# Per-head sums and spreads in 32-wide strips of TensorE, in a RWKV-7 mixer

## The chip, the cores and the metric

The kernel runs on one core of a Trainium2 chip, in one launch. The metric is the device time in microseconds (us). Each run gives one time; a profiled execution gives the rows that are quoted here. The engines are TensorE (PE; its weight loads are PEld), VectorE (DVE), ScalarE (ACT), GpSimd (POOL) and SyncE (SP), which issues the loads. Each works through its own queue in order, and waits for others by semaphores.

## The reference

One decoder layer over 256 tokens of width 2048: a mixer (pooling heads beside RWKV-7 heads), an MLP of width 8192, a gated embedding and a last norm. What the change touches are two places in the RWKV-7 half, which has 16 heads of 64 channels:

```python
kk = hs(k * k_k)                                  # (B, T, H, 64)
kk = kk / jnp.maximum(jnp.linalg.norm(kk, axis=-1, keepdims=True), 1e-12)
...
y = wkv7_scan(r_h, hs(decay), k_h, v_h, -kk, kk * a_h)
...                                               # group norm of y
y = y + jnp.sum(r_h * k_h * r_k, axis=-1, keepdims=True) * v_h
```

Both are a sum over the 64 channels of a head, for each token, and a spread of a number per head and token back over those channels: the inverse norm of kk, and the bonus that multiplies v.

## The kernel before

Activations of the mixer lie with channels on the 128 partitions and the 256 tokens along the free axis, as tiles of four 128-channel blocks: `[128, 4, 256]`, two heads in each block. The 16 heads are done in two groups of eight (`gi` 0 and 1), so a group is one such tile.

Products of the big weights are made of fp32r matmuls: ScalarE makes a rounded high part `wh` of the weights (L163), VectorE the rest `wl` (L164), and three matmuls per tile add high and low parts. An fp32 matmul, which the mixer's small work uses, stands in the profile as two passes, each with its own weight load.

TensorE's order is the order in which the code is written. Generators of the big products (`zk`, `zr`, `zv`, the pool's `zp`, and part of the output product, `o0a` and on) stand in a queue, and `fill(us)` takes steps from its head until about so many microseconds of matmuls are written; a step of `zk`, `zr` or `zv` is put at 0.36, one of `zp` at 0.68. So each `fill` is cover for what the small work waits for. The other engines' order is made by a scheduler, which goes by priorities (`tc.high_priority`) and its own estimates of time. `inverse` (a triangular inverse on VectorE, 31 steps on `X` and `tmp` and then four transposes, L661 and L665) is written beside the products.

The banks of PSUM for the small work come from a ring of four (`rw_bank`); the next user of a bank waits for its last reader.

The norms, in `rwkv_k`: ScalarE squares (L512, tile `tF`), TensorE sums a head's channels with the squares as the weights and two columns of ones, `jhead` (L524, tile `kkn`), so that tokens come out on the partitions: 128 x 16 numbers. VectorE and ScalarE make the inverse root `rn` (L527 to L529), TensorE transposes it (L533, `rnT`), it is split in high and low parts (`rnp`), and TensorE spreads it with `hsel` (L543, L544, tile `rnb`); VectorE multiplies (L548). The split parts borrow the place of `k2` (tag `tE`), so `k2` is made after them.

The bonus, in `rwkv_values`: v is transposed and centred (L699, `vt`; copies to `UV` at L701), then `block_sum` sums and spreads in one, by a 128 x 128 block of ones `jsum` (L463, `bsum`), and VectorE multiplies by v (L706).

The calls stand in this order: `rwkv_k(0)`, `rwkv_r(0)`, `rwkv_scores(0)`, inverse of group 0 beside, `rwkv_lora(1)`, `rwkv_k(1)`, `rwkv_r(1)`, the rest of the inverse, `rwkv_values(0)`, `fill(7.0)`, `rwkv_scores(1)`, and later `rwkv_merge(1)`, `rwkv_values(1)`, `rwkv_core(1)`.

Of the kernel before, what the change touches and what calls it, by code (L numbers as in the profile page):

```python
# [9 lines left out]
F32 = mybir.dt.float32  # L10
F32R = mybir.dt.float32r
AF = mybir.ActivationFunctionType
ALU = mybir.AluOpType
# [3 lines left out]
T = 256  # L17
# [23 lines left out]
def trunk(  # L41
# [19 lines left out]
    nc = tc.nc  # L61
# [7 lines left out]
    mc = rctx.enter_context(tc.tile_pool(name="mc", bufs=1))  # L69
# [4 lines left out]
    def rw_bank(name):  # L74
        return psr.tile([128, 512], F32, tag="rw", name=name)
# [5 lines left out]
    def col(name, j):  # L81
        o = PARAM_COLS[name] + j
        return par_sb[:, o : o + 1]
# [12 lines left out]
    jsum = mc.tile([128, 128], F32, name="jsum")  # L96
# [4 lines left out]
    nc.gpsimd.tensor_copy(jsum, cmask)  # L101
    cen = mc.tile([128, 128], F32, name="cen")
    nc.vector.scalar_tensor_tensor(cen, jsum, -1.0 / 64.0, ident, op0=ALU.mult, op1=ALU.add)
    jhead = mc.tile([128, 2], F32, name="jhead")
    nc.gpsimd.tensor_copy(jhead, cmask[:, ::64])
# [61 lines left out]
    def split_sb(h_ap, l_ap, src_ap):  # L167
        nc.scalar.activation(h_ap, src_ap, AF.Copy)
        nc.vector.tensor_tensor(l_ap, src_ap, h_ap.bitcast(F32), op=ALU.subtract)
# [67 lines left out]
    def advance():  # L237
        try:
            us = next(queue[0])
            pace(us)  # L240
            return us
        except StopIteration:
            queue.pop(0)
            return 0.0

    def fill(us):

        while us > 0 and queue:
            us -= advance()
# [47 lines left out]
    hsel_f = rp.tile([8, 512], F32, tag="BKt", name="hsel_f")  # L297
    nc.gpsimd.memset(hsel_f, 1.0)
    nc.gpsimd.affine_select(hsel_f, hsel_f, [[1, 512]], ALU.is_ge, 0.0, base=0, channel_multiplier=-64)
    nc.gpsimd.affine_select(hsel_f, hsel_f, [[-1, 512]], ALU.is_ge, 0.0, base=63, channel_multiplier=64)  # L300
    hsel = mc.tile([8, 512], F32R, name="hsel")
    nc.gpsimd.tensor_copy(hsel, hsel_f)

    def flat(t_):
        return t_.rearrange("p a t -> p (a t)")
# [148 lines left out]
    def pair_tile(tag, name, **kw):  # L454
        t_ = rp.tile([128, 2, 512], F32R, tag=tag, name=name, **kw)
        return t_[:, 0, :], t_[:, 1, :]

    def block_sum(src, name, consume):

        s = flat(src)  # L460
        for hf in range(2):
            b = rw_bank("bsum")
            nc.tensor.matmul(b, jsum, s[:, hf * 512 : (hf + 1) * 512], start=True, stop=True)  # L463
# [43 lines left out]
    def rwkv_k(gi, st, zk):  # L507
        P, EI, aa = st["P"], st["EI"], st["aa"]
        sq, kkn, k2 = e4("tF"), e4("tB"), e4("tE")
        with tc.high_priority(30000):  # L510
            for p in range(4):
                nc.scalar.activation(sq[:, p, :], zk[:, p, :], AF.Square, scale=col("k_k", 4 * gi + p))  # L512
        nc.scalar.activation(warm, sq[:, 3, 0:1], AF.Sqrt)

        fill(5.4)
        nb = rw_bank("kkn")
        for hf in range(2):
            h = flat(sq)[:, hf * 512 : (hf + 1) * 512]
            for j in range(2):
                for tt in range(2):  # L520
                    o = tt * 8 + (2 * hf + j) * 2
                    ts_ = slice(j * T + tt * 128, j * T + (tt + 1) * 128)
                    first = hf == 0 and j == 0 and tt == 0
                    nc.tensor.matmul(nb[:, o : o + 2], h[:, ts_], jhead, start=first, stop=True, skip_group_check=True)  # L524
        rn = rp.tile([128, 16], F32, tag="rn", name=f"rn{gi}")
        with tc.high_priority(30000):
            nc.vector.tensor_scalar_max(rn, nb[:, 0:16], 1e-24)  # L527
# [4 lines left out]
        for tt in range(2):  # L532
            nc.tensor.transpose(nb[0:8, tt * 128 : (tt + 1) * 128], rn[:, tt * 8 : tt * 8 + 8], ident)  # L533
        rnh, rnl = (t_[0:8, 0:T] for t_ in pair_tile("tE", f"rnp{gi}"))
        with tc.high_priority(30000):
            split_sb(rnh, rnl, nb[0:8, 0:T])
        fill(1.8)
        for half in range(2):
            b = rw_bank("rnb")
            for j in range(2):  # L540
                p = half * 2 + j
                o = b[:, j * T : (j + 1) * T]
                nc.tensor.matmul(o, hsel[:, p * 128 : (p + 1) * 128], rnh, start=j == 0, stop=False, skip_group_check=True)  # L543
                nc.tensor.matmul(o, hsel[:, p * 128 : (p + 1) * 128], rnl, start=False, stop=True, skip_group_check=True)  # L544
            for j in range(2):
                p = half * 2 + j
                with tc.high_priority(30000):
                    nc.vector.scalar_tensor_tensor(  # L548
                        kkn[:, p, :], zk[:, p, :], col("k_k", 4 * gi + p), b[:, j * T : (j + 1) * T], op0=ALU.mult, op1=ALU.mult
                )  # L550
# [140 lines left out]

    def rwkv_values(gi, st, zv):

        uvs = [rp.tile([128, 2, 8, 64], F32, tag=f"q{i}", name=f"UV{gi}_{i}") for i in range(2)]
        UV = [uvs[c // 2][:, c % 2] for c in range(4)]
        for tt in range(2):
            b = rw_bank("vt")
            for p in range(4):
                nc.tensor.matmul(b[:, p * 128 : (p + 1) * 128], zv[:, p, tt * 128 : (tt + 1) * 128], cen, start=True, stop=True)  # L699
            for i in range(2):  # L700
                nc.scalar.activation(flat3(UV[2 * tt + i])[64:128], b[i * 64 : (i + 1) * 64, :], AF.Copy)  # L701
        bon = st["rk"]
        bf, vf = flat(bon), flat(zv)
        block_sum(
            st["rk"], f"rk{gi}",
            lambda hf, b: nc.vector.tensor_tensor(  # L706
                bf[:, hf * 512 : (hf + 1) * 512], b, vf[:, hf * 512 : (hf + 1) * 512], op=ALU.mult
            ),
        )
        st["UV"] = UV  # L710

    def rwkv_core(gi, st):
# [88 lines left out]
    def flat3(t_):  # L801
        return t_.rearrange("s h i -> s (h i)")
# [588 lines left out]
```

## Time and profile before

| | us |
|---|---|
| median of 3 runs | 1205.14 (1204.48 to 1205.86) |
| profiled execution | 1204.86 |
| its span, first to last instruction | 1203.1 |
| TensorE busy | 1183.2 |
| VectorE busy | 872.9 |
| ScalarE busy | 674.7 |
| GpSimd busy | 15.5 |

The times of the profile count from the start of the span. A row of the order in time has start, duration, engine, line, operation, tiles (written from read), shapes and how many it merges; in square brackets stands how long the engine was idle before it and what ended that. Matmuls are pipelined: what one costs is the distance to the start of the next, not its duration. The mixer lies between 25 and 340 us, the first group's norms near 60, the second group's near 141 to 151, the values of the groups at 164 and 269.

### The profile page before, as it was taken

How to read it: one execution, taken by the hardware profiler on the slowest of the kernel's cores; microseconds unless marked ns; L12 is line 12 of the kernel's file. 1: busy time of each engine (PE TensorE's matmuls, PEld its weight loads, DVE VectorE, ACT ScalarE, POOL GpSimd, SP SyncE). 2: the span in 40 equal slices, each digit the busy share in tenths (PEclk: the TensorE clock that was granted, in tenths of full speed). 3: DMA queues.
4: the chain of work that ended last, by engine and by line, in shares of the span. 5: the costliest groups of instructions: out<-in, count | busy, mean ns of one | idle time of the engine just before them, and what ended most of it. 6: DMA issues, size and time to landing. Idle time of an engine off the chain costs nothing.

```text
span 1203.1 us, 18401 instructions
## 1 busy us (share of the span) xinstructions
PE 1183.2 (98%) x7070; PEld 1015.0 (84%) x7070; DVE 872.9 (73%) x1186; ACT 674.7 (56%) x1203; POOL 15.5 (1%) x65
## 2 busy tenths in 40 slices
PE   7999999999999999999999999999999999999997
PEld 5999988987888888888888888888888887887886
DVE  6887987964566666666878887666667788788753
ACT  5957556565545545555545554555555555468743
POOL 3100000000000000000000000000000000000000
PEclk9999999999999999999999999999999999999999
DMA  7363543354365565565656666665565666666841
GB/s 275 124 195 113 175 141 107 107 187 142 120 211 175 175 192 184 185 191 180 192 200 205 206 194 217 185 191 181 187 192 168 194 205 204 229 203 200 271 139 70
DMA packets 60616, 216.88 MB, mean 180 GB/s; under 512 B 6768, under 2 KB 7536, under 8 KB 60144
## 3 DMA queue, kind: packets, MB, share of 16 engines
q1 hardware_dynamic: 60240, 215.20, 55.5%
q8 instruction: 55, 0.90, 0.3%
q10 hardware_dynamic: 288, 0.51, 0.1%
q14 instruction: 33, 0.27, 0.1%
HBM read 213.59 MB, written 2.10 MB: 179 GB/s over the span
## 4 chain that ended last, share of the span: by engine, by line
PE 89%; DVE 6%; DMA 2%; ACT 2%; issue 1%; ACTq 0%; DVEq 0%
PE u_w L1016 20%; PE d_p L1085 15%; PE u_w L1020 10%; PE d_w L1085 4%; PE d_d L1085 4%; DMA raw_d<-in_w_ffn_down_dram 2%; PE gt_b L187 2%; PE gt_b L186 2%; PE gt_b L185 2%; PE wag_b L346 1%; PE zp_b L185 1%; PE zv_b L176 1%; PE zp_b L187 1%; PE zp_b L186 1%; PE o_b L186 1%; PE o_b L185 1%
## 5 line engine op out<-in xcount | busy, mean ns | idle before, releaser
L1016 PE MATMUL u_w<-h,wh_u 128*128 128x512 f32 x1024 | 362.1, 399 | 0.0
L1020 PE MATMUL u_w<-h,wl_u 128*128 128x256 f32 x1024 | 287.7, 281 | 0.0
L164 DVE TENSOR_TENSOR wl_u<-raw_u,wh_u 128x1024 fp32r<-128x1024 f32 x128 | 156.7, 1224 | 122.2 <-ACT wh_u L163 122.2
L163 ACT ACTIVATE wh_u<-raw_u 128x512 fp32r<-128x512 f32 x256 | 147.6, 624 | 173.4 <-issue 137.0
L1016 PEld LDWEIGHTS u_w<-h,wh_u 128*128 128x128 f32 x1024 | 192.4, 188 | 47.9
L1020 PEld LDWEIGHTS u_w<-h,wl_u 128*128 128x128 f32 x1024 | 193.4, 189 | 0.0
L1085 PE MATMUL d_p<-wh_d,yd 128*128 128x512 f32 x480 | 154.5, 389 | 0.8 <-ACT wh_d L163 0.8
L163 ACT ACTIVATE wh_d<-raw_d 128x512 fp32r<-128x512 f32 x160 | 89.1, 620 | 36.8 <-issue 18.5
L1085 PEld LDWEIGHTS d_p<-wh_d,yd 128*128 128x128 f32 x480 | 90.1, 188 | 20.0 <-ACT wh_d L163 1.2
L164 DVE TENSOR_TENSOR wl_d<-raw_d,wh_d 128x1024 fp32r<-128x1024 f32 x80 | 95.4, 1220 | 14.3 <-ACT wh_d L163 13.9
L1085 PE MATMUL d_p<-wl_d,yd 128*128 128x512 f32 x240 | 93.6, 390 | 0.0
L1085 PE MATMUL d_d<-wh_d,yd 128*128 128x512 f32 x160 | 55.8, 389 | 0.0
L1085 PEld LDWEIGHTS d_p<-wl_d,yd 128*128 128x128 f32 x240 | 45.1, 188 | 9.7 <-DVE wl_d L164 0.6
L1138 ACT ACTIVATE th_d<-t_d 128x1024 fp32r<-128x1024 f32 x24 | 25.4, 1058 | 47.6 <-DVE t_d L1135 30.2
L1085 PE MATMUL d_w<-th_d,ys 128*128 128x512 f32 x144 | 48.2, 389 | 0.0
L1142 ACT ACTIVATE th_d<-t_d 128x1024 fp32r<-128x1024 f32 x24 | 25.4, 1059 | 35.4 <-DVE t_d L1140 31.2
L1143 DVE TENSOR_TENSOR tl_d<-t_d,th_d 128x1024 fp32r<-128x1024 f32 x24 | 29.4, 1225 | 19.9 <-ACT th_d L1142 19.6
L1132 ACT ACTIVATE w7h_d<-raw_d 128x1024 fp32r<-128x1024 f32 x24 | 25.4, 1059 | 23.4 <-DMA raw_d<-in_w_ffn_down_dram 13.8
L187 PE MATMUL gt_b<-wh_gt,h 128*128 128x512 f32 x96 | 37.8, 393 | 0.0
L176 PE MATMUL zv_b<-hTh,wh_zv 128*128 128x256 f32 x128 | 37.7, 294 | 0.0
L176 PE MATMUL zr_b<-hTh,wh_zr 128*128 128x256 f32 x128 | 37.5, 293 | 0.0
L185 PE MATMUL gt_b<-wh_gt,h 128*128 128x512 f32 x96 | 37.5, 390 | 0.0
(582 smaller groups left out, 2622.8 us busy)
## 6 DMA issues: line engine op xcount, KB each, us to landing
raw_u<-in_w_ffn_up_dram SPq DMA_DIRECT2D x128, 512.0 KB, 3.5
raw_d<-in_w_ffn_down_dram SPq DMA_DIRECT2D x128, 512.0 KB, 3.9
raw_gt<-in_w_ple_gate_dram SPq DMA_DIRECT2D x24, 512.0 KB, 4.2
raw_zk<-in_w_in_dram SPq DMA_DIRECT2D x16, 512.0 KB, 3.4
raw_zr<-in_w_in_dram SPq DMA_DIRECT2D x16, 512.0 KB, 3.5
raw_zv<-in_w_in_dram SPq DMA_DIRECT2D x16, 512.0 KB, 3.4
raw_zp<-in_w_in_dram SPq DMA_DIRECT2D x16, 512.0 KB, 3.4
raw_o<-in_w_out_dram SPq DMA_DIRECT2D x16, 512.0 KB, 4.1
```

The lines of the kernel that those rows point to most:

```text
L163: nc.scalar.activation(wh[:, a * 512 : (a + 1) * 512], raw[:, a * 512 : (a + 1) * 512], AF.Copy)
L164: nc.vector.tensor_tensor(wl, raw, wh.bitcast(F32), op=ALU.subtract)
L176: nc.tensor.matmul(o, w_h, ah, start=first and ct % 2 == 0, stop=False, skip_group_check=True)
L185: nc.tensor.matmul(o, a_h, wh[:, 0:n], start=first, stop=False)
L186: nc.tensor.matmul(o, a_h, wl[:, 0:n], start=False, stop=False)
L187: nc.tensor.matmul(o, a_l, wh[:, 0:n], start=False, stop=last)
L1016: nc.tensor.matmul(bank[:, ct, :].rearrange("p (s t) -> p s t", s=2), wh[:, c], hl, start=k == 0, stop=False, skip_group_check=True,)
L1020: nc.tensor.matmul(bank[:, ct, 0:T], wl[:, c], hl[:, 0, :], start=False, stop=k == 15, skip_group_check=True)
L1085: nc.tensor.matmul(o, l, r, start=first, stop=last, skip_group_check=True)
L1132: nc.scalar.activation(ha, ra, AF.Copy)
L1138: nc.scalar.activation(th[0], t[0], AF.Copy)
L1143: nc.vector.tensor_tensor(tl[1], t[1], th[1].bitcast(F32), op=ALU.subtract)
```

## The change

The norms: the squares are now the moving operand, and the weights are 32 columns of `jsel`, zeros with two columns of ones (one for each head of a block) at a place that depends on the piece. Each block p writes its own 32 rows of the bank, so the four blocks use four strips of 32 columns of TensorE. The tokens are cut into eight pieces of 32, and piece q goes to rows 2q and 2q+1 of each strip: 128 x 32 numbers, 32 matmuls of 32 columns for 8 before. After the inverse root, VectorE multiplies `rn`, repeated eight times, by the mask `qmask`, which leaves each row only its own 32 tokens (`rnq`, 128 x 256). Four fp32 matmuls, each in a strip of 32 rows with a bank of its own, spread it over the channels by `hsel`. The transpose, the split and the two fills of 3.2 and 1.8 around it are gone; one `fill(5.0)` stands in their place. `k2` no longer waits for the split.

The bonus: the same sums in one piece (four matmuls of 256 columns), a ScalarE copy `bs`, a `fill(1.5)`, four spread matmuls, and four VectorE products instead of two. All this stands ahead of `vt` now, and was behind it. Masks are made on GpSimd at the start; `jsum` and `jhead` are gone.

```diff
-    def block_sum(src, name, consume):
-
-        s = flat(src)
-        for hf in range(2):
-            b = rw_bank("bsum")
-            nc.tensor.matmul(b, jsum, s[:, hf * 512 : (hf + 1) * 512], start=True, stop=True)
-            consume(hf, b)
+    def head_sums(src, name, pieces):
+
+        b = rw_bank(name)
+        n = T // pieces
+        for q in range(pieces):
+            for p in range(4):
+                nc.tensor.matmul(
+                    b[p * 32 : (p + 1) * 32, 0:n], jsel[:, 14 - 2 * q : 46 - 2 * q], src[:, p, q * n : (q + 1) * n],
+                    start=q == 0, stop=q == pieces - 1, skip_group_check=True,
+                )
+        return b[:, 0:n]
+
+    def head_spread(src, name):
+
+        banks = [rw_bank(f"{name}{p}")[:, 0:T] for p in range(4)]
+        for p in range(4):
+            r = slice(p * 32, (p + 1) * 32)
+            nc.tensor.matmul(banks[p], hsel[r], src[r], start=True, stop=True)
+        return banks
...
-        nb = rw_bank("kkn")
...
-        rn = rp.tile([128, 16], F32, tag="rn", name=f"rn{gi}")
+        nb = head_sums(sq, "kkn", 8)
+        rn = rp.tile([128, 32], F32, tag="rn", name=f"rn{gi}")
+        rnq = rp.tile([128, T], F32, tag="sq", name=f"rnq{gi}")
...
             nc.vector.reciprocal(rn, rn)
-        fill(3.2)
-        nb = rw_bank("rnT")
...
-        fill(1.8)
-        for half in range(2):
-            b = rw_bank("rnb")
...
+            nc.vector.tensor_tensor(
+                rnq.rearrange("r (q t) -> r q t", q=8), rn.unsqueeze(1).to_broadcast([128, 8, 32]), qmask, op=ALU.mult
+            )
+        fill(5.0)
+        rnb = head_spread(rnq, "rnb")
...
     def rwkv_values(gi, st, zv):
 
+        bon = st["rk"]
+        nb = head_sums(bon, "bsum", 1)
+        bs = rp.tile([128, T], F32, tag="sq", name=f"bs{gi}")
+        with tc.high_priority(30000):
+            nc.scalar.activation(bs, nb, AF.Copy)
+        fill(1.5)
+        for p, b in enumerate(head_spread(bs, "bon")):
+            with tc.high_priority(30000):
+                nc.vector.tensor_tensor(bon[:, p, :], b, zv[:, p, :], op=ALU.mult)
...
-        block_sum(
-            st["rk"], f"rk{gi}",
...
-        )
```

What this does to the order of instructions is seen at three places. First TensorE around `rwkv_values(0)`, before: the end of the product zr of the second group, the transposes of v, the sums, and the first step of the pool's product.

```order
L178 MATMUL zr_b_1653<-hTh_158,wl_zr_7_1944 128x256
L699 MATMUL vt<-cen,zv_t 128x128 x8
L463 MATMUL bsum<-ybuf,jsum 128x512 x2
L185 MATMUL zp_b_2022<-wh_zp_0_2026,hTh_157 128x512
L186 MATMUL zp_b_2022<-wl_zp_0_2027,hTh_157 128x512
L187 MATMUL zp_b_2022<-wh_zp_0_2026,hTl_159 128x512
```

And after: the sums (row 1053 of that queue) are followed by three steps of the pool's product, of which the last is shown, and then this.

```order
L184 MATMUL zp_b_2072<-wh_zp_0_2076,hTh_156 128x512
L185 MATMUL zp_b_2072<-wl_zp_0_2077,hTh_156 128x512
L186 MATMUL zp_b_2072<-wh_zp_0_2076,hTl_158 128x512
L479 MATMUL bon_2090<-bs_2070,hsel 128x256
L479 MATMUL bon_2091<-bs_2070,hsel 128x256
L479 MATMUL bon_2092<-bs_2070,hsel 128x256
L479 MATMUL bon_2093<-bs_2070,hsel 128x256
L706 MATMUL vt<-cen,zv_t 128x128 x8
```

The spread of the bonus stands between the pool's product and vt, and takes a bank for each block.

Second, ScalarE at the same place, before: the splits of zp, the evacuations of zr (L309), the copies back of the inverse (L669, `SC` from `tmp`) and the copies of vt.

```order
L309 ACTIVATE zr_t<-zr_b_1652,omu 128x256 [waits PE_49]
L163 ACTIVATE wh_zp_2_2064<-raw_zp_2_2062 128x512 [waits DMAHW2_49,DVE_49,PE_49]
L309 ACTIVATE zr_t<-zr_b_1653,omu 128x256 [waits PE_49]
L309 ACTIVATE zr_t<-zr_b_1652,omu 128x256 [waits DVE_49]
L163 ACTIVATE wh_zp_2_2064<-raw_zp_2_2062 128x512
L669 ACTIVATE SC_1054<-tmp_1232 32x32x32 [waits DVE_49]
L309 ACTIVATE zr_t<-zr_b_1653,omu 128x256 [waits DVE_49]
L669 ACTIVATE SC_1054<-tmp_1232 32x32x32
L701 ACTIVATE UV_1_2001<-vt 64x512 [waits PE_49,Pool_49]
```

And after:

```order
L667 ACTIVATE SC_1101<-tmp_1279 32x32x32 [waits DVE_49]
L667 ACTIVATE SC_1101<-tmp_1279 32x32x32
L313 ACTIVATE zr_t<-zr_b_1699,omu 128x256 [waits PE_49]
L313 ACTIVATE zr_t<-zr_b_1700,omu 128x256 [waits PE_49]
L696 ACTIVATE bs_2070<-bsum 128x256 [waits PE_49]
L162 ACTIVATE wh_zp_2_2142<-raw_zp_2_2140 128x512 [waits DMAHW2_49,Activation_49]
L313 ACTIVATE zr_t<-zr_b_1699,omu 128x256 [waits DVE_49]
L313 ACTIVATE zr_t<-zr_b_1700,omu 128x256 [waits DVE_49]
L162 ACTIVATE wh_zp_2_2142<-raw_zp_2_2140 128x512
L708 ACTIVATE UV_1_2103<-vt 64x512 [waits PE_49,Pool_49]
```

The new copy bs stands behind both SC copies and two of the four evacuations of zr.

Third, VectorE in `rwkv_k(1)`, before: the last steps of the inverse, its first two transposes, the low part of the norms, a split, a transpose, and the four products with the spread norms.

```order
L656 TENSOR_TENSOR X_1231<-X_1231,tmp_1232 64x31
L661 STREAM_TRANSPOSE T1G_1993<-X_1231 32x16x32 x2
L169 TENSOR_TENSOR rnp_1783<-rnT,rnp_1783 8x256
L164 TENSOR_TENSOR wl_zr_5_1876<-raw_zr_5_1873,wh_zr_5_1875 128x1024
L665 STREAM_TRANSPOSE tmp_1232<-X_1231 64x16x32
L548 SCALAR_TENSOR_TENSOR tB_t<-zk_t,par_sb,rnb 128x256 x4
```

And after, from behind the last but one zk_t to the masked norms:

```order
L654 TENSOR_TENSOR X_1278<-X_1278,tmp_1279 64x25x7
L163 TENSOR_TENSOR wl_zr_2_1811<-raw_zr_2_1808,wh_zr_2_1810 128x1024
L314 SCALAR_TENSOR_TENSOR zk_t<-zk_b_1384,par_sb,zk_t 128x255
L650 TENSOR_TENSOR tmp_1279<-X_1278,AT_1277 64x156
L553 TENSOR_TENSOR tE_t<-tE_t,zk_t 128x1024
L163 TENSOR_TENSOR wl_zr_3_1846<-raw_zr_3_1843,wh_zr_3_1845 128x1024
L566 TENSOR_TENSOR BK_1888<-tE_t,tC_t 128x16x64
L536 TENSOR_SCALAR rn_1802<-kkn 128x32
L163 TENSOR_TENSOR wl_zr_4_1906<-raw_zr_4_1903,wh_zr_4_1905 128x1024
L538 RECIPROCAL rn_1802<-rn_1802 128x32
L654 TENSOR_TENSOR X_1278<-X_1278,tmp_1279 64x26x6
L539 TENSOR_TENSOR rnq_1803<-rn_1802,qmask 128x256
```

The products of k2 (tE, BK) and a split have moved ahead of the norms, a split now stands between the last two zk_t, and the last steps and the transposes of the inverse come after the spread.

More of the change, by code (lines that the diff above doesn't have):

```diff
@@ L95, in trunk @@
     nc.vector.memset(ones, 1.0)
-    jsum = mc.tile([128, 128], F32, name="jsum")
     cmask = mc.tile([128, 128], F32, name="cmask")
@@ L100, in trunk @@
     make_block_diagonal(nc, cmask, 64)
-    nc.gpsimd.tensor_copy(jsum, cmask)
     cen = mc.tile([128, 128], F32, name="cen")
-    nc.vector.scalar_tensor_tensor(cen, jsum, -1.0 / 64.0, ident, op0=ALU.mult, op1=ALU.add)
-    jhead = mc.tile([128, 2], F32, name="jhead")
-    nc.gpsimd.tensor_copy(jhead, cmask[:, ::64])
+    nc.vector.scalar_tensor_tensor(cen, cmask, -1.0 / 64.0, ident, op0=ALU.mult, op1=ALU.add)
+    jsel = mc.tile([128, 46], F32, name="jsel")
+    nc.gpsimd.memset(jsel, 0.0)
+    nc.gpsimd.tensor_copy(jsel[:, 14:16], cmask[:, ::64])
     for r0 in (0, 64):
@@ L295, in e4 @@
         return rp.tile([128, 4, T], F32, tag=tag, name=f"{tag}_t")
[L297 to L302, printed above, removed]
+    hsel = mc.tile([128, 128], F32, name="hsel")
+    nc.gpsimd.memset(hsel[0:32], 0.0)
+    for q in range(8):
+        nc.gpsimd.affine_select(hsel[0:32], hsel[0:32], [[-1, 2], [0, 64]], ALU.not_equal, 1.0, base=-2 * q, channel_multiplier=1)
+    qmask = mc.tile([128, 8, 32], F32, name="qmask")
+    nc.gpsimd.memset(qmask[0:32], 1.0)
+    nc.gpsimd.affine_select(qmask[0:32], qmask[0:32], [[-2, 8], [0, 32]], ALU.is_ge, 0.0, base=0, channel_multiplier=1)
+    nc.gpsimd.affine_select(qmask[0:32], qmask[0:32], [[2, 8], [0, 32]], ALU.is_ge, 0.0, base=1, channel_multiplier=-1)
+    for p in range(1, 4):
+        nc.gpsimd.tensor_copy(hsel[p * 32 : (p + 1) * 32], hsel[0:32])
+        nc.gpsimd.tensor_copy(qmask[p * 32 : (p + 1) * 32], qmask[0:32])
     def flat(t_):
@@ L515, in rwkv_k @@
         fill(5.4)
-        nb = rw_bank("kkn")
[L517 to L524, printed above, removed]
@@ L531, in rwkv_k @@
-        nb = rw_bank("rnT")
[L532 to L536, printed above, removed]
-        fill(1.8)
-        for half in range(2):
-            b = rw_bank("rnb")
[L540 to L549, printed above, removed]
+            nc.vector.tensor_tensor(
+                rnq.rearrange("r (q t) -> r q t", q=8), rn.unsqueeze(1).to_broadcast([128, 8, 32]), qmask, op=ALU.mult
+            )
@@ L550, in rwkv_k @@
+        fill(5.0)
+        rnb = head_spread(rnq, "rnb")
+        for p in range(4):
+            with tc.high_priority(30000):
+                nc.vector.scalar_tensor_tensor(
+                    kkn[:, p, :], zk[:, p, :], col("k_k", 4 * gi + p), rnb[p], op0=ALU.mult, op1=ALU.mult
                 )
```

8 lines of the change are left out of this document (2 added, 6 removed).

## The prediction

> **What bounds the kernel now.** I read the page first (busy shares, then the chain that ended last), then the stretches of the mixer, then the order in time of TensorE, VectorE and ScalarE around the lines that the change touches.
>
> ```profile
> PE 1183.2 (98%) x7070; PEld 1015.0 (84%) x7070; DVE 872.9 (73%) x1186; ACT 674.7 (56%) x1203; POOL 15.5 (1%) x65
> PE 89%; DVE 6%; DMA 2%; ACT 2%; issue 1%; ACTq 0%; DVEq 0%
> ```
>
> TensorE is busy 98% of the span and carries 89% of the chain, so time taken from it, or a wait added to it, moves the end one for one. The 6% of VectorE lie in the mixer:
>
> ```profile
> 120.00:140.00 20.00, 19.93 (x167) 19.72 (x166) 19.28 (x41) 10.45 (x20) 0.00 (x0) 1.00 0.55 177
> 140.00:160.00 20.00, 19.20 (x144) 18.48 (x143) 19.12 (x34) 12.23 (x24) 1.10 (x2) 0.91 0.46 155
> 152.00:155.40 3.40, 3.40 (x19) 3.40 (x19) 3.40 (x6) 1.86 (x5) 0.00 (x0) 0.52 0.36 133
> ```
>
> The columns are length, TensorE, weight loads, VectorE, ScalarE, GpSimd, granted clock, DMA. From 120 to 160 us VectorE is busy 19.28 and 19.12 of 20 us (it runs the first inverse beside the weight splits), so there it is nearly the bound. And TensorE loses something there that no busy number tells: the granted clock falls to 0.52 from 152.0 to 155.4, just after this wait:
>
> ```profile
> 147.31 2.00 DVE L661 STREAM_TRANSPOSE T1G<-X 32x512 f32<-32x512 f32 x2
> ...
> 148.56 0.38 PE L543 MATMUL rnb<-rnp,hsel 8*128 8x256 f32 x1
> 149.61 0.38 PE L544 MATMUL rnb<-rnp,hsel 8*128 8x256 f32 x1 [0.67 <-DVE rnp L169]
> ```
>
> The second spread matmul starts 1.05 us after the first instead of about 0.12, because the low half of the norms stood on VectorE behind two transposes of the inverse. That is 0.95 us lost, and in the half-clock stretch 19 matmuls run where 28 fit (3.40 / 0.12), another 1.1 us.
>
> **The change part by part.** Setup: more small GpSimd work (13 rows more), done long before its first use at 59 us; GpSimd is 1% busy, so 0. VectorE computes cen a few rows earlier among the squares, where it waits for a load anyway: 0.
>
> TensorE work of one group, by starts before, in the first group and (values) in the second half:
>
> ```profile
> 58.90 0.28 PE L178 MATMUL zr_b<-hTh,wl_zr 128*128 128x256 f32 x1
> 59.02 1.84 PE L524 MATMUL kkn<-jhead,tF_t 128*128 128x2 f32 x16
> 60.72 0.36 PE L176 MATMUL zr_b<-hTh,wh_zr 128*128 128x256 f32 x1
> ...
> 64.04 0.38 PE L533 MATMUL rnT<-ident,rn 128*8 128x128 f32 x2
> 64.17 0.36 PE L176 MATMUL zr_b<-hTh,wh_zr 128*128 128x256 f32 x1
> ...
> 66.28 0.28 PE L178 MATMUL zr_b<-hTh,wl_zr 128*128 128x256 f32 x1
> 66.49 0.38 PE L543 MATMUL rnb<-rnp,hsel 8*128 8x256 f32 x1
> ...
> 67.62 0.39 PE L176 MATMUL zr_b<-hTh,wh_zr 128*128 128x256 f32 x1
> 67.84 0.28 PE L177 MATMUL zr_b<-hTl,wh_zr 128*128 128x256 f32 x1
> ...
> 164.09 1.95 PE L699 MATMUL vt<-cen,zv_t 128*128 128x128 f32 x16
> 165.87 1.88 PE L463 MATMUL bsum<-ybuf,jsum 128*128 128x512 f32 x4
> 167.82 0.40 PE L186 MATMUL zp_b<-wl_zp,hTh 128*128 128x512 f32 x1
> 168.05 0.40 PE L187 MATMUL zp_b<-wh_zp,hTl 128*128 128x512 f32 x1
> ```
>
> A product matmul takes 0.12 from start to start (58.90 to 59.02). kkn costs 60.72 - 59.02 = 1.70: eight fp32 matmuls, two passes each. rnT costs 0.13 and slows the next by about 0.08: 0.21. rnb runs from 66.40 to 67.84 less one pitch: 1.32. The bsum of a group (four passes, 0.43 each) runs from 165.87 to 167.82 less the first product's own 0.23 (167.82 to 168.05): 1.72. A step of the 512-wide products is three of these, 0.69.
>
> What replaces them is not in the trace: 64 passes with 32 columns for the norms (K), 8 passes of 256 columns in four column strips for the bonus (M), and twice 8 passes of 256 in four row strips (S). The nearest rows are passes that already run in two strips, and 32x32 ones in a single strip:
>
> ```profile
> 45.07 0.48 PE L491 MATMUL lw<-zf,wa 64*128 64x256 f32 x1
> 45.08 0.48 PE L491 MATMUL la<-zf,wa 64*128 64x256 f32 x1
> ...
> 45.83 0.38 PE L491 MATMUL la<-zf,wa 64*128 64x256 f32 x1
> 46.14 0.39 PE L176 MATMUL zk_b<-hTh,wh_zk 128*128 128x256 f32 x1
> ...
> 262.36 2.21 PE L680 MATMUL gm<-T1G,SC 32*32 32x32 f32 x64
> 264.50 0.50 PE L185 MATMUL zp_b<-wh_zp,hTh 128*128 128x512 f32 x1
> ...
> 280.03 0.69 PE L767 MATMUL sm<-UV,BKt 128*64 128x64 f32 x16
> 280.55 1.10 PE L780 MATMUL rym<-UV,SC 128*64 128x64 f32 x16
> ```
>
> lw and la, in two strips of 64 rows, start 0.01 apart: strips do run beside each other, 8 passes of 256 in 46.14 - 45.07 = 1.07. sm does the same with two column strips: 16 passes in 0.52, 0.033 each, where the 16 of rym in one strip show 1.10. gm, one strip, takes 2.14 / 64 = 0.033. So for K: no overlap gives 2.14, two strips at a time 1.07, four 0.53; I take 1.15, the two-strip row that is shown plus a start. For M and S: no overlap 1.73 (eight halves of a bsum pass), two strips 1.07, four 0.53; I take 0.8, since rows 45.07 and 45.08 show no sign of a limit at two. By the Trainium skill, "TensorE: Matmul & The Clock Gate", section on the 56 ns gap, matmuls never start closer than about 25 ns however few their columns; as an estimate from it K would be 1.6 and the sum 0.45 higher. No row here can settle that: sm and gm average 0.033.
>
> First group: K saves 0.55, rnT 0.21, S 0.52: **-1.28**. It passes on whole, since the inverse that loads VectorE afterwards is itself started by TensorE's scores.
>
> Second group. Here the order on the other engines changes more than the work does, and two waits are new. I keep the clock of before and set the -1.28 aside.
>
> ```profile
> 139.66 0.86 DVE L310 SCALAR_TENSOR_TENSOR zk_t<-zk_b,par_sb,zk_t 128x255 f32<-128x255 f32 x2
> 159.59 1.23 DVE L164 TENSOR_TENSOR wl_zp<-raw_zp,wh_zp 128x1024 fp32r<-128x1024 f32 x1 [0.57 <-ACT wh_zp L163]
> ...
> 162.99 1.22 DVE L164 TENSOR_TENSOR wl_zp<-raw_zp,wh_zp 128x1024 fp32r<-128x1024 f32 x1
> 164.13 0.48 DVE L310 SCALAR_TENSOR_TENSOR zr_t<-zr_b,par_sb,zr_t 128x255 f32<-128x255 f32 x1
> 164.60 1.15 DVE L665 STREAM_TRANSPOSE tmp<-X 64x512 f32<-64x512 f32 x1
> 170.65 1.27 DVE L706 TENSOR_TENSOR ybuf<-bsum,zv_t 128x512 f32<-128x512 f32 x2
> ...
> 139.89 1.30 ACT L512 ACTIVATE tF_t<-zk_t,par_sb 128x256 f32<-128x256 f32 x3
> 155.40 1.15 ACT L163 ACTIVATE wh_zr<-raw_zr 128x512 fp32r<-128x512 f32 x2 [1.54 <-PE zr_b L177]
> 164.70 0.82 ACT L309 ACTIVATE zr_t<-zr_b,omu 128x256 f32<-128x256 f32 x2
> 165.93 1.04 ACT L669 ACTIVATE SC<-tmp 32x1024 f32<-32x1024 f32 x1
> 167.35 1.06 ACT L669 ACTIVATE SC<-tmp 32x1024 f32<-32x1024 f32 x1
> ```
>
> First wait: the sums now take all four squares in their first four matmuls, while before the first half of kkn took two. The last square was ready at 141.19. Now a split (1.14, from 162.99 to 164.13) stands ahead of the last zk_t on VectorE, and one (1.15) ahead of the last square on ScalarE: about 142.6. TensorE arrives at 140.71 and waits 1.9. Then K to 143.75, 14 product steps of 0.36 to 148.8 (the 0.95 wait is gone: after 139.66 VectorE has five rows of 1.14 and eight short ones of together 2.5 up to the masked norms, 147.9), S to 149.6, 34 steps to 161.85, M to 162.65, three steps of 0.69 to 164.7. If the clock halves after the 1.9 wait, 165.8.
>
> Second wait: the spread of the bonus needs bs, a ScalarE copy, and ScalarE now has it behind the two SC copies, which need the last transposes of the inverse. Those ended on VectorE at 165.75; one split (1.14) and one zr_t (0.4) leave the rows ahead of them, which gives 164.2, or 163.6 without the 0.57 of idle at 159.59; I take 164.0. Two SC copies (2.0) to 166.0, two zr_t (0.82) to 166.8, bs (0.45) to 167.3. TensorE, there at 164.7 to 165.8, waits 1.5 to 2.6. Who is late next: the spread takes all four banks, so vt has to wait until VectorE has multiplied the first. VectorE has four zr_t and two r k rows ahead, and the third zr_t waits for ScalarE's, behind bs and half a split: about 168.3. Two zr_t to 169.1, the product to 169.55. vt then runs 1.78 to 171.4. Before, the same place was reached at 167.6, plus the three steps that now lie inside (2.05): 169.65. So **+1.75**, nearly whatever TensorE does ahead of it.
>
> The half clock after that: two waits of together three us or more in five, where 0.95 sufficed at 148.6, cost one more stretch like 152.0 to 155.4: **+1.1**. The row shows half clock after a wait of one microsecond.
>
> Values of the second group: M + S - 1.72 = -0.12, and vt waits for the first product (0.43, and some 0.15 to start): **+0.45**. bs is covered there by three product steps. Everything behind (merges, core, pool, MLP) is the same work in shifted order: 0.
>
> Sum against the profiled execution, which took 1204.86 with a span of 1203.1: 1204.86 - 1.28 + 1.75 + 1.1 + 0.45 = 1206.9. The median of the runs is 0.28 above the profiled time; I say **1207.0**, its own range 1205 to 1209.
>
> **Rivals.** *No half clock.* The waits come, but the clock stays up: the sum without its 1.1, 1205.8. For it: the price of a wait is known from one place alone. Against: 0.95 us sufficed at 148.6. Chance 0.13. By the Trainium skill, the same page, Part 1, the clock falls after an idle window of about 3.4 us, and neither wait is that long; the trace does not agree at 152.0.
>
> *The waits stay away* (other side). If VectorE came to the last transposes 2.6 us sooner, bs would be there at 164.7 and TensorE would never wait in the values: vt would end at 164.7 + 0.8 + 1.78 = 167.3 against 169.65, so -2.35, no half clock, and 1204.86 - 1.28 - 2.35 + 0.45 = 1201.7. It decides at bs: each microsecond that it comes sooner than 167.3 is one less. For it: VectorE had some idle there before. Against: 19.12 busy of 20. Chance 0.14.
>
> *Two stretches of half clock*, and the one after the first wait reaches the rows that VectorE waits for: +1.1 and +0.8, 1208.8. For it: the waits fall within five microseconds and can spoil two windows. Chance 0.25.
>
> *The strips do not do what they say*: no more overlap in fours than in one. K 2.14, S and M 1.73: the first group turns from -1.28 to +0.64, the second values from +0.45 to +1.75, and 0.5 more before the second sums: 1210.6. Rows 45.07 and 280.03 speak against it. Chance 0.12.
>
> **From these the numbers.** The forecast has 0.36, the rivals 0.13, 0.14, 0.25 and 0.12. Faster or slower by 0.2%, 2.4 us, is about what a measurement of this kernel can tell from none. Below 1202.7 lies most of the first rival and a little of the forecast's tail: 0.15. Above 1207.5 lie the last two and a small part of the forecast: 0.39. Between: 0.46. The range runs from 1202.0 (the first rival at its edge) to 1210.5 (nearly the third).
>
> **What would show it.** Right: kkn starting and stopping once near 140 us for about 2 us; TensorE idle ahead of bon in the first values on ScalarE's bs, and ahead of vt on VectorE's product; a stretch of half clock between 165 and 176. Each K, M, S is read from starts in the first group and the second values. Wrong: bs ready before TensorE asks, VectorE idle between 150 and 165, or S near 1.7.

## The result, and the profile after

| | before | after |
|---|---|---|
| median of the runs, us | 1205.14 | 1209.31 |
| after / before, 95% interval | | 1.0043 [1.0025, 1.0061] |
| the same kernels in a later comparison | 1204.88 | 1209.17, 1.0031 [1.0020, 1.0042] |
| profiled execution, us | 1204.86 | 1208.33 |
| its span | 1203.1 | 1206.6 |
| first lora matmul to first MLP matmul (u_w) | 348.8 | 351.7 |

The changed kernel is slower by 0.3 to 0.4%. The last line is what the rest of this text goes by: the mixer from its first `lw` to the first matmul of the MLP. It takes out when that `lw` starts (45.07 and 44.15 here, 44.0 to 45.6 in all the profiles). What follows the mixer took between 806.7 and 811.2 us in the 14 profiles seen here, whatever was changed, so the times scatter by that as well. Each mixer is read from one profile; the only kernel that was profiled twice, the changed one, gave 351.7 and 351.9.

The page of the changed kernel, busy shares and chain: no engine has more to do but GpSimd, and TensorE is even 2.5 us less busy. Its share of the chain fell from 89% to 57%; what took its place was not followed up.

```profile
PE 1180.7 (98%) x7186; PEld 1010.8 (84%) x7186; DVE 872.5 (72%) x1190; ACT 674.3 (56%) x1203; POOL 21.2 (2%) x79
PE 57%; DVE 10%; DMA 6%; ACT 2%; issue 2%; DVEq 0%; ACTq 0%
```

The stretches show where it went (length, TensorE, weight loads, VectorE, ScalarE, GpSimd, granted clock, DMA, GB/s).

```profile
120.00:140.00 20.00, 18.50 (x157) 18.05 (x155) 19.45 (x38) 12.43 (x26) 0.00 (x0) 1.00 0.50 169
140.00:160.00 20.00, 19.97 (x220) 18.88 (x221) 19.76 (x34) 8.53 (x15) 1.10 (x2) 1.00 0.46 159
160.00:180.00 20.00, 16.51 (x85) 13.20 (x84) 13.00 (x21) 10.91 (x21) 0.00 (x0) 0.83 0.36 130
164.00:170.90 6.90, 5.51 (x27) 4.67 (x28) 6.34 (x13) 2.54 (x7) 0.00 (x0) 0.54 0.27 101
```

From 120 to 140 TensorE is busy 18.50 for 19.93 before: two waits, of 0.5 and 1.0. From 140 to 160 it is better than before: 19.97 for 19.20, and clock 1.00 for 0.91. From 160 to 180 TensorE lacks 3.5 us, and the clock is 0.83: from 164.5 to 171.3, twice 3.41 us, it is a half. Before, it had been busy throughout there, at the full clock:

```profile
160.00:180.00 20.00, 20.00 (x129) 16.54 (x129) 16.79 (x23) 11.96 (x23) 0.00 (x0) 1.00 0.43 142
```

All waits of TensorE from 25 to 345 us:

```profile
PE bon L479 <- ACT bs L696: 2.3, 1, 2.3
PE vt L706 <- DVE ybuf L700: 1.2, 1, 1.2
PE kkn L468 <- ACT tF_t L528: 1.0, 1, 1.0
PE vt L706 <- DVE tF_t L700: 0.9, 1, 0.9
PE zk_b L177 <- DVE wl_zk L163: 0.5, 1, 0.5
PE rym L737 <- DVE sbd L777: 0.5, 1, 0.5
```

Before, the only one there was the 0.7 at rnb, which is gone. TensorE in order of time, at the norms of both groups and in the first values:

```profile
58.19 0.76 PE L468 MATMUL kkn<-tF_t,jsel 128*32 128x32 f32 x64
58.88 0.39 PE L175 MATMUL zr_b<-hTh,wh_zr 128*128 128x256 f32 x1
...
64.10 0.71 PE L479 MATMUL rnb<-rnq,hsel 32*128 32x256 f32 x8
64.74 0.39 PE L175 MATMUL zr_b<-hTh,wh_zr 128*128 128x256 f32 x1
...
138.75 0.26 PE L468 MATMUL kkn<-tF_t,jsel 128*32 128x32 f32 x6
140.03 0.71 PE L468 MATMUL kkn<-tF_t,jsel 128*32 128x32 f32 x58 [1.02 <-ACT tF_t L528]
...
158.97 0.64 PE L468 MATMUL bsum<-ybuf,jsel 128*32 128x256 f32 x8
159.54 0.50 PE L184 MATMUL zp_b<-wh_zp,hTh 128*128 128x512 f32 x1
...
164.17 0.95 PE L479 MATMUL bon<-bs,hsel 32*128 32x256 f32 x8 [2.27 <-ACT bs L696]
166.34 3.79 PE L706 MATMUL vt<-cen,zv_t 128*128 128x128 f32 x16 [1.22 <-DVE ybuf L700]
169.78 0.77 PE L184 MATMUL zp_b<-wh_zp,hTh 128*128 128x512 f32 x1
```

The strips are cheap: 64 passes of the sums in 0.69, the spread in 0.64, the sums of the bonus in 0.57. The first values, 158.97 to 169.78, are not. VectorE and ScalarE meanwhile:

```profile
158.65 2.17 DVE L663 STREAM_TRANSPOSE tmp<-X 64x512 f32<-64x512 f32 x2
...
163.51 0.87 DVE L314 SCALAR_TENSOR_TENSOR zr_t<-zr_b,par_sb,zr_t 128x255 f32<-128x255 f32 x2 [1.63 <-ACT zr_t L313]
...
165.88 1.40 DVE L700 TENSOR_TENSOR ybuf<-bon,zv_t 128x256 f32<-128x256 f32 x4
...
160.85 2.13 ACT L667 ACTIVATE SC<-tmp 32x1024 f32<-32x1024 f32 x2 [3.61 <-DVE tmp L663]
163.00 0.84 ACT L313 ACTIVATE zr_t<-zr_b,omu 128x256 f32<-128x256 f32 x2
163.73 0.38 ACT L696 ACTIVATE bs<-bsum 128x256 f32<-128x256 f32 x1
```

ScalarE stands 3.61 us, since the two SC copies, which need the inverse's last transposes (158.65 to 160.8), are ahead of everything else in its queue. Then come zr_t and bs. VectorE in its turn stands 1.63 for zr_t, and makes the first product only after four of them and two r k rows (L583). TensorE asks for bs at about 161.9 and for the product at about 165.1.

### The profile page after: what moved, and what is told of

Same layout as the page of the kernel before. It is cut to its first block, busy times and chain, and to the rows that moved or that the text cites. A ratio compares the mean times of both kernels' runs of the same rounds, so it can differ in the third digit from the quotient of the medians.

```text
span 1206.6 us, 18653 instructions
## 1 busy us (share of the span) xinstructions
PE 1180.7 (98%) x7186; PEld 1010.8 (84%) x7186; DVE 872.5 (72%) x1190; ACT 674.3 (56%) x1203; POOL 21.2 (2%) x79
## 4 chain that ended last, share of the span: by engine, by line
PE 57%; DVE 10%; DMA 6%; ACT 2%; issue 2%; DVEq 0%; ACTq 0%
PE u_w L1015 20%; PE u_w L1019 10%; PE d_p L1084 6%; DMA raw_d<-in_w_ffn_down_dram 6%; DVE wl_d L163 2%; PE gt_b L186 2%; PE gt_b L185 2%; PE gt_b L184 2%; PE d_w L1084 2%; PE d_d L1084 2%; DVE w7l_d L1132 1%; DVE tl_d L1140 1%; PE o_b L184 1%; PE o_b L185 1%; PE o_b L186 1%
## 5 line engine op out<-in xcount | busy, mean ns | idle before, releaser
L185 PE MATMUL gt_b<-wl_gt,h 128*128 128x512 f32 x96 | 37.4, 390 | 0.0
```

The costliest lines, as they stand in the source:

```text
L185: nc.tensor.matmul(o, a_h, wl[:, 0:n], start=False, stop=False)
```

## The experiments

Each was measured beside the kernel before on the same chip, in four comparisons; the median of before was 1204.22 in the first (the first four lines), 1204.40 in the second (the next four), 1204.55 in the third and 1204.88 in the last (the changed kernel again). "Mixer" is the stretch of the first table: before 348.8, after 351.7 (again 351.9).

| kernel | ratio to before, 95% | mixer |
|---|---|---|
| norms alone | 0.9974 [0.9963, 0.9984] | 344.5 |
| values alone | 1.0013 [1.0005, 1.0022] | 350.7 |
| vt between sums and spread | 1.0029 [1.0018, 1.0040] | 351.4 |
| more cover ahead of the spread | 1.0034 [1.0022, 1.0047] | 351.5 |
| vt first, spread late | 1.0024 [1.0015, 1.0034] | 351.3 |
| norms alone, one strip at a time | 0.9987 [0.9978, 0.9996] | 345.7 |
| before, with cover at rnb | 0.9987 [0.9976, 0.9999] | 346.4 |
| spread late, kkn later | 1.0024 [1.0012, 1.0035] | 351.0 |
| bs ahead of SC | 1.0024 [1.0014, 1.0035] | 350.6 |
| whole bonus early | 0.9973 [0.9964, 0.9983] | 345.1 |
| norms alone, kkn later | 0.9977 [0.9966, 0.9987] | 344.3 |
| changed kernel again | 1.0031 [1.0020, 1.0042] | 351.9 |

**The two halves.** First the norms as after with `block_sum` and the old values.

```diff
-        nb = head_sums(bon, "bsum", 1)
...
-        for p, b in enumerate(head_spread(bs, "bon")):
+        block_sum(
+            st["rk"], f"rk{gi}",
...
```

> The norms as in the changed kernel, the values (sums, spread, vt) as in the kernel before. Theory A, the values lose what the norms gain: the norms bring TensorE to the first values about 4 us sooner (158.97 against 164.09, with a start that was 0.91 earlier), and vt there needs nothing that is late, so 1201 to 1202.5 and no half clock after 157. Rival B, the inverse on VectorE is the bound there and TensorE only waits later, at the scores or the merge: 1204 to 1205.5, with one new wait of 2 to 4 us on VectorE or on SC. Rival C, the loss is in the norms (K, S dear, the wait of 1.0 before kkn): 1207 or more.

Measured 1201.32, theory A. The stretch has no idle TensorE and the full clock:

```profile
160.00:180.00 20.00, 20.00 (x121) 15.41 (x120) 16.58 (x24) 14.36 (x30) 0.00 (x0) 1.00 0.53 160
```

In order of time, vt and the sums run at once:

```profile
158.87 1.95 PE L707 MATMUL vt<-cen,zv_t 128*128 128x128 f32 x16
160.66 1.88 PE L469 MATMUL bsum<-ybuf,jsum 128*128 128x512 f32 x4
...
169.08 1.28 DVE L714 TENSOR_TENSOR ybuf<-bsum,zv_t 128x512 f32<-128x512 f32 x2
```

The products come at 169.08, three us later than in the changed kernel, and nobody waits: the sums lie in two banks, behind vt. Then the other half, the old norms with the new values:

```diff
-        nb = head_sums(sq, "kkn", 8)
+        nb = rw_bank("kkn")
...
```

> The norms as before, the values as in the changed kernel. Theory A with the inverse's end as the fixed point: TensorE comes to the values 4 to 5 us later than in the changed kernel, so bs is nearly there when the spread is reached (wait 0 to 0.7), vt still waits about 1.2 for VectorE's product: 1205.5 to 1207.5. Rival C, the strips M and S in themselves are the loss: 1208 to 1210, with starts that show it. Rival D, the waits depend on the order alone and not on when TensorE arrives: bon waits 2.3 as in the changed kernel, 6.8 us of half clock, 1209 to 1210.

Measured 1205.9. This is the time of theory A. Waits of vt 0.7 and 0.9, no wait for bs, no half clock of the values. But the reason is another than theory A gave:

```profile
164.72 0.38 ACT L718 ACTIVATE bs<-bsum 128x256 f32<-128x256 f32 x1
...
165.86 2.11 ACT L689 ACTIVATE SC<-tmp 32x1024 f32<-32x1024 f32 x2
...
166.33 0.71 PE L483 MATMUL bon<-bs,hsel 32*128 32x256 f32 x8
167.73 2.05 PE L728 MATMUL vt<-cen,zv_t 128*128 128x128 f32 x16 [0.69 <-DVE ybuf L722]
```

Theory A took the inverse's end as fixed. It is not: the SC copies come 5.0 us later than in the changed kernel (165.86 for 160.85). With the old norms ScalarE has bs and zr_t ahead of them, with the new ones behind them. So the halves don't add up: by the mixer -4.3 and +1.9 alone, together +2.9. I read the missing 5.3 as the order that the schedule took on ScalarE when both came together, and the clock that fell on the waits. That is argued and not shown: no run turned that order alone, and the one below that put bs ahead of SC, with zr_t still behind, won 1.1 of it.

**Cover in the values.** Two kernels, one with vt and its copies ahead of the `fill(1.5)` of the values:

```diff
+        uvs = [rp.tile(...) for i in range(2)]
+        ...
         fill(1.5)
         for p, b in enumerate(head_spread(bs, "bon")):
...
-        uvs = [rp.tile(...) for i in range(2)]
-        ...
```

> The changed kernel with vt and its copies to UV between the sums and the spread of the bonus. Theory A: vt (1.8 us) runs while ScalarE has bs still to make, so the wait for bs falls from 2.3 to about 0.5 and vt's own wait (1.2) is gone: 1205.5 to 1207.5. Rival E, the ring of four banks: the spread then waits for the UV copies on ScalarE, which stand behind SC and bs: the wait only changes its name, 1208.5 to 1210.

And one with more cover there, the same products moved ahead:

```diff
-        fill(1.5)
+        fill(6.0 if gi == 0 else 1.5)
...
-    fill(7.0)
+    fill(2.5)
```

> The changed kernel with fill 6.0 for 1.5 ahead of the first spread of the bonus and 2.5 for 7.0 behind vt (the same products, about six steps or 4.1 us moved ahead). Theory A: the wait for bs (2.3) is gone and so are most of the half clock and vt's wait: 1205 to 1206.5. Rival B, VectorE is late there by itself: a wait of 1 to 3 us at the second scores, which have lost their cover: 1208 to 1209.5.

Measured 1208.14 and 1208.94: rival E by its wait, 0.4 below its range, and rival B by its time, though the wait is not at the second scores. Both found a new thing to wait for. With vt ahead:

```profile
PE bon L479 <- ACT UV L704: 2.3, 1, 2.3
PE bon L479 <- ACT bs L696: 0.4, 1, 0.4
```

With more cover (the wait for bs is gone):

```profile
PE vt L706 <- DVE ybuf L700: 2.0, 1, 2.0
PE zp_b L185 <- DVE wl_zp L163: 1.7, 1, 1.7
```

The spread takes four banks of a ring of four. With vt ahead it needs banks that wait for UV copies; with vt behind, vt needs the product. And cover made of zp steps asks VectorE for their weights' low parts, which are late there too.

**The spread later.** vt, sums and bs in the values, the spread 5.5 us on.

```diff
     rwkv_values(0, st0, zv0[0])
-    fill(7.0)
+    fill(5.5)
+    rwkv_bonus(0, st0, zv0[0])
+    fill(1.5)
```

> The changed kernel with the values taken apart: vt first, then the strip sums and bs, and the spread with its products only behind 5.5 (group 0, the 7.0 ahead of the second scores split into 5.5 and 1.5) or behind the 1.5 that stands ahead of the core (group 1, whose own 1.5 goes). Theory A, the loss is the early date at which the values ask for bs and for the four banks: no wait of TensorE on bs or on vt, no half clock near 165, and the strips (measured 0.57 and 0.64, against 1.72 for the sums before) save 0.5 in each group: 0.5 to 1 below the kernel with the norms alone (1201.3), 1200 to 1201.5. Rival E, the ring of four banks: the spread waits for UV copies or the scores for the products, 1 to 2 us in each group: 1203 to 1205.

Measured 1207.87, rival E, and worse than its price:

```profile
171.05 0.69 PE L479 MATMUL bon<-bs,hsel 32*128 32x256 f32 x2 [2.27 <-DVE ybuf L712]
...
170.58 0.42 DVE L712 TENSOR_TENSOR ybuf<-bon,zv_t 128x256 f32<-128x256 f32 x1
```

Three spreads ran, the fourth waited for the first product. Only three banks were to be had: one half of vt stays in its bank until after the merge, since its copy goes to the place that the inverse's T1G still holds (tag `q0`; so in the code), and comes at 197.80, after the merge's matmuls, where the other half's came at 166.24. The clock fell to a half twice, for 3.41 us each. With three steps moved ahead of the sums of the norms as well:

```diff
-        fill(5.4)
+        fill(5.4 if gi == 0 else 6.5)
         nb = head_sums(sq, "kkn", 8)
...
-        fill(5.0)
+        fill(5.0 if gi == 0 else 3.9)
```

> The kernel with vt first and the late spread, and in the second group three product steps moved from behind the sums of the norms to ahead of them (6.5 and 3.9 for 5.4 and 5.0). Theory A and the wait for the fourth square (1.02 at 140): that wait is gone, 0.8 to 1.0 below the kernel with the late spread alone: 1199.2 to 1200.5. Rival B, VectorE is the bound near 140 (19.45 and 19.76 of 20 us busy): rnb then waits for rnq by 0.5 to 1, and nothing is won, or a half clock comes in: the same as the late spread alone or up to 1.5 above it.

Measured 1207.19, mixer 351.0 for 351.3: rival B, the wait for the square turned into this one:

```profile
PE rnb L479 <- DVE rnq L539: 0.7, 1, 0.7
```

**What the strips give.** The norms alone, with the loops of `head_sums` changed over.

```diff
-        for q in range(pieces):
-            for p in range(4):
+        for p in range(4):
+            for q in range(pieces):
```

> The kernel of the norms alone, with the 32 sums in the other order: all eight pieces of block 0, then of block 1 and so on, so that 16 passes in a row use one strip. Theory F, the four strips overlap because neighbours in order use different strips: the 64 passes grow from 0.69 to 1.7 to 2.2 in each group, while the wait of 1.0 for the fourth square in the second group shrinks by what the first three blocks take: the first group is slower by 1.0 to 1.5, the second equal: 1202 to 1203. Rival G, passes of 32 columns are cheap in any order: 0.7, the wait shrinks to about 0.5, 1200.5 to 1201.3.

Measured 1202.74, theory F:

```profile
58.55 1.91 PE L478 MATMUL kkn<-tF_t,jsel 128*32 128x32 f32 x64
60.40 0.39 PE L177 MATMUL zr_b<-hTh,wh_zr 128*128 128x256 f32 x1
```

The same 64 passes take 1.85 for 0.69: 0.029 each in one strip, 0.011 when neighbours use four. The new order also lets neighbours add up in the same rows of the bank, and no run parts the two; the gm row of the prediction, one strip without such sums, has 0.033. Next, the kernel before, with no strip at all:

```diff
-        fill(1.8)
+        fill(1.8 if gi == 0 else 3.2)
```

> The kernel before with 3.2 for 1.8 ahead of the spread of the norms in the second group (four more product steps of 0.36 as cover, the work the same). Theory H, a part of the norms' gain comes from no strip at all but from the wait for rnp (0.95 with what it delays) and the half clock after it (3.41 us at half, 1.7): no wait at rnb, no half clock near 152, 2 to 2.7 below before: 1201.5 to 1202.3. Rival I, VectorE is behind by itself: the 0.7 reappears at rnb or the gain is lost at the next wait (values, scores): 1203.5 to 1204.5.

Measured 1202.59, 1.8 below before: theory H by what the trace shows, 0.3 above its range. The wait is gone and the clock stays up:

```profile
140.00:160.00 20.00, 19.89 (x165) 19.37 (x163) 19.69 (x35) 14.95 (x28) 1.10 (x2) 1.00 0.50 158
```

So 2.4 of the 4.3 us that the new norms save in the mixer are to be had with one number. That leaves 1.9, by subtraction, for the strips and the transpose that is gone. From start to start, kkn, rnT and rnb of both groups take 5.9 us in this run, and 2.9 in the norms alone without the wait at kkn. So the work saves 3.0, and the two waits that come with the new norms, 1.0 at kkn and 0.5 at zk, take half of that back.

**Where the values wait.** bs of the first group made early, ahead of SC, the rest in its place.

```diff
     rwkv_k(1, st1, zk1[0])
+    fill(3.0)
+    bs0 = rwkv_sums(0, st0)
     finish(p_zr1)
```

> The changed kernel with the sums of the first group's bonus and the copy bs moved ahead, to three us behind the norms of the second group, so that bs stands ahead of the SC copies on ScalarE; spread, products and vt stay where they were. Theory A as the runs so far have bent it (VectorE itself is what is late: it is busy 19.8 of 20 us there, and the first product stands behind four zr_t): bon no longer waits (2.3 gone), but vt waits 3 to 4 for the product, which comes no sooner: 1208 to 1209.5, half clock as in the changed kernel. Rival J, bs behind the SC copies is the cause: both waits go, 1202 to 1204.

Measured 1208.32: the time of theory A; of its half clock only one stretch.

```profile
151.83 0.39 ACT L695 ACTIVATE bs<-bsum 128x256 f32<-128x256 f32 x1 [2.08 <-PE bsum L468]
...
162.94 0.71 PE L479 MATMUL bon<-bs,hsel 32*128 32x256 f32 x8
...
167.25 3.13 PE L712 MATMUL vt<-cen,zv_t 128*128 128x128 f32 x13 [3.60 <-DVE ybuf L706]
...
162.09 2.12 ACT L667 ACTIVATE SC<-tmp 32x1024 f32<-32x1024 f32 x2 [2.95 <-DVE tmp L663]
164.24 0.84 ACT L313 ACTIVATE zr_t<-zr_b,omu 128x256 f32<-128x256 f32 x2
...
164.75 0.87 DVE L314 SCALAR_TENSOR_TENSOR zr_t<-zr_b,par_sb,zr_t 128x255 f32<-128x255 f32 x2 [1.62 <-ACT zr_t L313]
...
166.78 1.41 DVE L706 TENSOR_TENSOR ybuf<-bon,zv_t 128x256 f32<-128x256 f32 x4
```

The spread is done before 164 and VectorE stands idle up to 164.75, but the products are behind four zr_t in its queue, and those behind the SC copies on ScalarE. So the expectation's reason, that VectorE has too much work, does not hold at this spot: it has an order. Rival J, bs alone, is out as well: TensorE's wait for bs went, and its wait for the product grew from 1.2 to 3.6.

**The whole bonus early.** Sums, bs, spread and products at about 108 us (first group) and 252 us (second), where nothing that they need is late; only vt stays.

```diff
     finish(p_zv0)
+    fill(1.0)
+    rwkv_bonus(0, st0, zv0[0], 1.8)
+    fill(2.0)
     st1 = rwkv_lora(1)
...
     finish(p_zv1)
-    fill(4.0)
+    fill(1.0)
+    rwkv_bonus(1, st1, zv1[0], 1.5)
+    fill(1.5)
```

> The changed kernel with the whole bonus (strip sums, bs, spread, products) taken out of the values and put early: for the first group between the end of its zv and the second lora (among 1.0, 1.8 and 2.0 of the second zk), for the second group behind its zv (the 4.0 there split in 1.0, 1.5 and 1.5); only vt stays in the values. Theory A: nothing in the values asks for VectorE or for banks, so no wait there and no half clock; the strips stay, and save about 0.5 in each group against the old sums: 1200 to 1201.5, at or below the kernel of the norms alone. Rival K, any product more on VectorE before the inverse's end delays what follows (kkn, rnb, wl_zp), so that the waits turn up near 140 and 160: 1203 to 1206.

Measured 1201.45, theory A. All waits of TensorE over 0.2 us from 25 to 345 us:

```profile
PE zr_b L177 <- DVE wl_zr L163: 0.6, 1, 0.6
PE zk_b L177 <- DVE wl_zk L163: 0.4, 1, 0.4
```

The strips' half microsecond in each group does not show against the norms alone (345.1 for 344.5). The wait of 1.0 at kkn shrank to 0.1 here, but zk and zr together take 2.0 us more from start to start (78.9 for 76.9), 0.8 of it in waits for the low parts; the rest was not followed up. The last kernel, the norms alone with two steps moved ahead of their sums:

```diff
-        fill(5.4)
+        fill(5.4 if gi == 0 else 6.1)
...
-        fill(5.0)
+        fill(5.0 if gi == 0 else 4.3)
```

> The kernel of the norms alone, with two product steps of the second group moved from behind the strip sums to ahead of them (6.1 and 4.3 for 5.4 and 5.0). If the wait of 1.02 for the fourth square is a plain loss: 0.5 to 0.7 below 1201.3. If VectorE is the bound near 140 (the run with both showed rnb waiting 0.7 for rnq when three steps were moved): rnb waits 0.3 to 0.5, and the time is that of the norms alone within 0.4.

Measured 1201.13 beside 1204.55. The wait for the square fell from 1.0 to 0.6 and rnb did not wait, so neither of the two expectations came as written; the mixer gained 0.2, which the times cannot tell.

**Once more the changed kernel.**

> The changed kernel as it is, a second profile and more times. In its first profile the mixer's end is 2.9 us later than before (counted from the first lora), and 1.5 us more came behind the mixer, where nothing was changed (TensorE waits for d_p of 2.0 against 0.8). If those belong to the change: the same waits near 590 and 1080, and 1.0043 again. If they are the spread of runs: other waits there, a profile within 0.3 of the first up to the mixer's end (bon 2.3, vt 1.2, 6.8 us of half clock), and a ratio of 1.0025 to 1.0035 like the other kernels that wait in the values.

Measured 1209.17, ratio 1.0031. The waits of the mixer are the same to 0.1 (2.3, 1.2, 1.0, 0.9) and so are the 6.83 us of half clock. The 2.0 at d_p are 0.3 here. What follows the mixer took 810.4, in the first profile 810.8 and before 809.3, all within the scatter given above, so none of it can be laid to the change.

## Why the prediction came out as it did

Forecast 1207.0, measured 1209.31: slower, as forecast, above the forecast's own 1205 to 1209 and inside the whole range, 1202.0 to 1210.5. The likeliest outcome by the chances, a difference under 0.2% (0.46), did not come; slower had 0.39. The places were right, and what happened is nearest to the rival *Two stretches of half clock* (1208.8). That 1209.31 lies so near to it is in part luck: of the 2.3 us beyond the forecast 0.9 lie in the mixer, and the rest lies outside it, where the runs scatter (the second comparison gives 1.0031, 3.7 us, with the same mixer). By the steps, in the mixer:

| step | forecast | measured |
|---|---|---|
| K, S, M (us of TensorE) | 1.15, 0.8, 0.8 | 0.69, 0.64, 0.57 |
| first group | -1.28 | -1.60 |
| kkn(1) waits for the fourth square | 1.9 | 1.02 |
| TensorE waits for bs | 1.5 to 2.6 | 2.27 |
| from the first scores to the second (waits and half clock) | +2.85 | +3.43 |
| values of the second group | +0.45 | +0.60 |
| core of the first group | 0 | +0.48 |
| sum | +2.02 | +2.91 |

The measured rows are distances between markers in the two profiles, less the 2.07 of the three zp steps that moved in. First lora to first scores: 41.82 before, 40.22 after. First to second scores: 88.32 and 93.82. First qm of the second group to the first rym of its core: 7.93 and 10.60. First rym of the first core to its gt: 42.24 and 42.72.

*The strips* were over-priced. For K I took the two-strip row plus a start, for S and M a value between two strips and four, where four strips run. Together 0.6 cheaper in the first group, they moved it by 0.3 only: the products around a small block start 0.2 apart instead of 0.12, which I charged to the old rows alone, and the same shows around the strips (64.74 to 64.97). The rival that they do nothing is out (K would be 2.14). By the Trainium skill, "TensorE: Matmul & The Clock Gate", section "Wait — 56ns, not 53.3ns?", starts are never closer than about 25 ns; the trace agrees for neighbours in one strip (0.029) and disagrees for four (0.011), and the estimate K 1.6 falls with it.

*The waits.* Both are where the working put them, for its reason: bs behind the SC copies, vt behind the product since the spread takes all banks. But one sign of being wrong did show: VectorE idle between 150 and 165, 1.63 us. There it was held by the order on ScalarE and not by its own load. And the inverse's last transposes ended 0.7 us sooner than worked out (160.8; the 164.0 of the working is 161.5 here, less the earlier start and what the first group saved), and so did the product (165.9 for 166.6). Counted so, vt would have ended 1.0 later than before at the full clock, where +1.75 was forecast. The rival that the waits stay away is out for this order; its time, 1201.7, is about what two kernels reached that do not ask there, but not in its way, by a sooner VectorE.

*The half clock* is the term that was mis-sized: one stretch for 1.1 was forecast, two came. vt took 3.44 in them (166.34 to 169.78) where the norms alone show 1.79 (158.87 to 160.66), and the first zp step 1.43 for 0.69: 2.4 us. With the 1.0 above that makes the 3.43 of the table: the half clock cost 1.3 more than forecast, and the sooner product gave about 0.75 of it back. The 1.1 was too low for one stretch as well. The row 152.00:155.40 begins before the stretch (152.15 to 155.56), and its 19 counts matmuls that only reach into it; from start to start the 16 in the stretch take 0.213 each for 0.12, together 1.5 more. The price was read from one place, rnb, and does not carry over: the wait of 1.02 at kkn was followed by no half clock at all.

*Not foreseen* is the core's first group, +0.48. rym waits 0.5 for sbd, a state that VectorE makes. I had put everything behind the values at 0. The same wait is there with the values alone, and not with the norms alone.

*One reading was wrong* without moving the sum: of the chain's 6% of VectorE before, about 70 us, only half lies in the mixer, nearly all of it from 100 to 160 us. The other half lies from 1020 to 1100 us, behind the MLP's first product.

## What to carry to other kernels

Price a new intermediate (sum, copy, spread, product) by the place in each queue that it will stand in, not by its work: here 1.7 us of matmuls became 1.2 and cost the mixer 2 us alone and 7 beside the new norms (344.5 to 351.7), since in-order queues had other work ahead of it. A tile that several results share for long, here a ring of four banks, turns an asker that does not wait into one that does; count the banks held when a spread wants all of them. And try the small move first: a few steps of cover at an existing wait gave half of what the rewritten norms gave (2.4 of 4.3), and the bonus was harmless at a place where its inputs had long been ready.

## What the runs showed of the hardware

- Matmuls of 32 columns in four column strips start 0.011 us apart on average, and 0.029 when neighbours use the same strip. Fp32 passes of 256 columns run four abreast as well: 8 in 0.57 with column strips, 8 in 0.64 with row strips.
- Half clock came, inside the kernels, in stretches of 3.41 us, or twice that. A wait of 3.6 us in the values was followed by one, two waits of 2.27 and 1.22 by two on end, the 0.67 at the 8-row rnb by one, and 0.68 at gm (32 x 32 matmuls, both kernels with the spread late) by one. The 1.02 at kkn was followed by none, nor was 0.68 at the 32-row rnb (spread late, kkn later); with more cover, a wait of 1.68 (zp) and one of 2.02 (vt), which end 3.4 us apart, had one stretch behind the second. By the Trainium skill, "TensorE: Matmul & The Clock Gate", Part 1, a free-running window of about 3.4 us decides and the clock falls after an idle one; the length agrees, but no window here was idle throughout when 0.67 or 2.27 sufficed. What counts as idle stays open: a wait's length alone does not tell.
